# Gate products of a recurrence one product later, and a Newton step in two operations

## The chip, the cores and the metric

The kernel runs on one core of a Trainium2 chip. The metric is the device time of one execution in microseconds, as the median of several runs. A core has TensorE (PE, matrix products into PSUM banks), VectorE (DVE), ScalarE (ACT), GpSimd (POOL) and SyncE (SP), which here only starts DMAs. Each engine works through its own queue in program order; semaphores tie the queues together.

## The reference

One layer of a decoder block on x of 2048 positions by 1024 features, in float32:

```python
proj = x @ w_in + b_in        # 1024 -> 9216 columns: q, k, v, g_attn, u_lru, g_lru, two merge gates
attn = combined(dilated_band_attention(rope(q), rope(k), v)) * silu(g_attn)   # three dilation groups
y_a  = attn @ w_attn_proj
u    = causal_depthwise_conv(u_lru, conv_w, conv_b)     # width 4
h    = rg_lru(u, ...)                                    # below
y_b  = (h * silu(g_lru)) @ w_lru_proj
out  = (sigmoid(gA) * y_a + sigmoid(gB) * y_b) @ w_out + b_out
x    = layer_norm(2 ** 0.25 * x + out, ln_gain, ln_bias)
```

The recurrence, with block-diagonal 64 x 64 gate weights:

```python
r = sigmoid(u @ w_r + b_r);  i = sigmoid(u @ w_i + b_i)
a = exp(-8 * r * softplus(-lam))
h[t] = a[t] * h[t-1] + sqrt(1 - a[t]**2) * i[t] * u[t]
```

## The kernel before

Every float32 product is made of three matmuls in the reduced-precision form `float32r`: an operand is split into a high part (ScalarE copies it into that form) and the rest (VectorE subtracts), and high x high, high x low and low x high are summed in PSUM.

**Stages.** The kernel runs four stages: the input projection with everything that can be done on its columns (to about 1446 us), attention (to about 1659 us), the projection of the recurrence's branch, and the attention projection with the output projection and LayerNorm (to the end).

**The input projection.** It is computed by Strassen's scheme (Winograd's form): two column tiles (of 128 columns) against two position chunks (of 512) make a *unit* of seven products instead of eight. There are 36 units in each half of the positions; `plan` lists them, and `seq` gives the order of kinds ("qk", "v", "ug" for the recurrence's input and its gate, "ga", "mg"). A product is 12 matmuls of 128 x 512 at line 622 and fills one PSUM bank `q`, of which there are four (line 615). The usual order of the products is `MID`, by their ids 1, 6, 7, 5, 2, 4, 3. After each product `evacuate` reads its bank: id 1 is copied by ScalarE to `e`; id 6 gives `u = e - q`, id 7 `v = u + q`, id 5 gives an output from `v` and then `u = u + q`, and ids 2, 4 and 3 give the other outputs. The weights' sums S1 to S4 (`add_w`, `sums`, `sum3`) and their splits (`prep_w`, writing `h` and `l`) are issued at fixed products ahead of use, their loads (`load_w`, line 234) earlier still.

**The chains.** What happens to an output afterwards is a Python generator, started in `result`: `qk_chain` (rotary, split, stores at lines 330, 341 and 344, with four DMAs at line 307 for the swapped halves), `v_chain`, `silu_chain`, `mg_chain` and `lru`. A chain yields `Ask(lag=.., need=.., keep=.., cond=.., ACT=.., DVE=..)`: its next step is issued `lag` products later at the earliest, when enough of the 32 slots of 128 x 512 are vacant, the condition holds, and the planner's budget of each named engine (2.75 us for every product) is not used up. The order that results in each queue is fixed when the program is built. `pe_later(n, fn)` puts matmuls of a chain into the middle of the product n on (line 625).

**The recurrence.** `lru(i, c, ub)` handles block i (of 8) and chunk c (of 4), 32 chains in all. It computes the convolution `v`, splits it into `vh` and `vl` (lines 482 and 483, the latter recorded under line 227), and two products later asks for the gates: `gates` issues six matmuls on half the rows each (line 492) into two banks `g`. Then follow the tanh of both gates on ScalarE, the coefficients, and the scan (line 527). `gate["busy"]` lets one chain at a time be between its gates and its tanh, and `gate["live"]` lets two chains be between convolution and scan.

**LayerNorm.** `out_job(tt)` handles 128 positions: the output product (lines 1415 to 1417), the residual, mean and variance, and then r = 1/sqrt(var + eps): ScalarE takes the root, VectorE the reciprocal (line 1443), and one Newton step r <- r * (1.5 - 0.5 * (var + eps) * r * r) corrects it, on one column of 128 values (lines 1445 to 1448). The two halves of the tile are then scaled, shifted (line 1452) and stored.

Of the kernel before, what the change touches and what calls it, by code (L numbers as in the profile page):

```python
# [11 lines left out]
ALU = mybir.AluOpType  # L12
# [19 lines left out]
def hybrid_block_kernel(ctx: ExitStack, tc: tile.TileContext, a: dict, out: bass.AP):  # L32
    nc = tc.nc
    sp, act, dve, pool, pe = nc.sync, nc.scalar, nc.vector, nc.gpsimd, nc.tensor
# [62 lines left out]
    def pe_later(lag, fn):  # L97
        pe_late.append((now["n"] + lag, fn))
# [348 lines left out]
    def lru(i, c, ub):  # L447
# [19 lines left out]
        for j in range(1, 4):  # L467
            dve.scalar_tensor_tensor(out=v, in0=ub[:, j:j + CH], scalar=lrn[:, j, i:i + 1], in1=v,
                                     op0=ALU.mult, op1=ALU.add)
# [24 lines left out]
            if c in ((0, 3) if i in put_off else (1, 3)):  # L494
                give(GW[i])

        pe_later(1, gates)
        gated[i] = c + 1
        yield Ask(lag=2, need=2, keep=1, ACT=2.5)
        gate["busy"] = False  # L500
        tr, ti = take("tr" + nm, F32), take("ti" + nm, F32)
        for h, (hs, os) in enumerate((HALF, HALF[::-1])):
# [69 lines left out]
    def result(s, fi, c, bank, u):  # L572
# [10 lines left out]
        if kind in ("qk", "v"):  # L583
            y = take("y" + nm)
            total(flat(y), bank, u, f, sgn, True)
            start_chain(qk_chain(y, f, c) if kind == "qk" else v_chain(y, sgn, f, c))
        elif kind == "mg":
            y = take("y" + nm, F32)
            total(y, bank, u, f, sgn, False)
            start_chain(mg_chain(y, sgn, f, c))  # L590
        elif kind == "ga" or not fi:
            y = take("y" + nm, F32)
            total(y, bank, u, f, sgn, False)
            start_chain(silu_chain(y, sgn, f, c))
        else:
            i = f - FT_U
            if c == 1 and i in put_off:
                y = take("y" + nm, F32)
                total(y, bank, u, f, sgn, True)
                act.activation(ubs[:, i, 2, 0:3], y[:, CH - 3:CH], AF.Copy)  # L600
                start_chain(store_chain(y, u_scr[i]))
                return
            ub = ub_free.pop(0)
            total(ub[:, 3:3 + CH], bank, u, f, sgn, True)
            start_chain(lru(i, c, ub), 7 if c % 2 else 0)
# [100 lines left out]
    for s, pl in enumerate(plan):  # L706
        if pl[4] == "ug" and not (pl[0] and pl[1][1][0] - FT_U in put_off):
            at(base[s] + 1, lambda i=pl[1][1][0] - FT_U: fetch_gr(i))
        if pl[0] and pl[4] == "ug":
            i = pl[1][1][0] - FT_U  # L710
            if i not in put_off:
                continue
            at(base[s] - 12, lambda i=i: start_chain(lru(i, 1, None)))
# [677 lines left out]
    def load_xr(tt):  # L1391
        XR[tt] = vx_p.tile([P, D], F32, tag="x", name=f"x{tt}", bufs=3)
        sp.dma_start(XR[tt], a["x"][tt * P:(tt + 1) * P, :])

    def split_m(tt, ks=slice(0, 8)):
        c, b = divmod(tt, 4)
        m = ME[c][:, ks, b * P:(b + 1) * P]
        if ks.start == 0:
            MS[tt] = tuple(vx_p.tile([P, 8, P], F32R, tag=t, name=f"{t}{tt}", bufs=2) for t in ("mh", "ml"))
        mh, ml = (t[:, ks] for t in MS[tt])  # L1400
        act.activation(mh, m, AF.Copy)
        dve.tensor_tensor(out=ml, in0=m, in1=flat(mh), op=ALU.subtract)

    def out_job(tt):
        rows = slice(tt * P, (tt + 1) * P)
        x = XR.pop(tt)
        mh, ml = MS.pop(tt)
        last = tt == 15
        parts = [slice(0, CH), slice(CH, CH + 256), slice(CH + 256, D)] if last else [slice(0, CH), slice(CH, D)]
        zz = [fp.tile([P, CH], F32, tag="z", name=f"z{tt}{n}", bufs=3)[:, 0:hs.stop - hs.start] for n, hs in enumerate(parts)]  # L1410
        for k0, k1 in ((0, 6), (6, 8)) if tt == 0 else ((0, 8),) if tt % 4 else ((0, 7), (7, 8)):
            for z, hs in zip(zz, parts):
                for k in range(k0, k1):
                    w = WO[k]
                    pe.matmul(z, mh[:, k], w[:, 0, hs], start=(k == 0), stop=False)  # L1415
                    pe.matmul(z, mh[:, k], w[:, 1, hs], start=False, stop=False)  # L1416
                    pe.matmul(z, ml[:, k], w[:, 0, hs], start=False, stop=(k == 7))  # L1417
        if tt + 1 < 16:
            load_xr(tt + 1)
            split_m(tt + 1, slice(0, 8 if (tt + 1) % 4 else 7))  # L1420
        if tt == 1:
            for fn in at1:
                fn()
        dve.scalar_tensor_tensor(out=x, in0=x, scalar=ALPHA, in1=vec[0], op0=ALU.mult, op1=ALU.add)
        st_ = cst.tile([P, 4, 6], F32, tag="st", name=f"st{tt}", bufs=2)
        n = 0
        for z, hs in zip(zz, parts):
            dve.tensor_tensor(out=x[:, hs], in0=x[:, hs], in1=z, op=ALU.add)
            step = 256 if last else CH
            for q in range(hs.start, hs.stop, step):  # L1430
                dve.bn_stats(out=st_[:, n, :], in_=x[:, q:q + step])
                n += 1
        mv = cst.tile([P, 4], F32, tag="mv", name=f"mv{tt}", bufs=2)
        dve.bn_aggr(out=mv[:, 0:2], in_=st_[:, 0:n])
        act.activation(mv[:, 2:3], mv[:, 1:2], AF.Sqrt, bias=epst)
        halves = (slice(0, CH), slice(CH, D))

        def centre(hs):
            dve.scalar_tensor_tensor(out=x[:, hs], in0=x[:, hs], scalar=mv[:, 0:1], in1=vec[1][:, hs],
                                     op0=ALU.subtract, op1=ALU.mult)  # L1440

        centre(halves[0])
        dve.reciprocal(out=mv[:, 2:3], in_=mv[:, 2:3])

        dve.tensor_scalar(out=mv[:, 1:2], in0=mv[:, 1:2], scalar1=EPS, scalar2=-0.5, op0=ALU.add, op1=ALU.mult)
        dve.tensor_tensor(out=mv[:, 3:4], in0=mv[:, 2:3], in1=mv[:, 2:3], op=ALU.mult)
        dve.tensor_scalar(out=mv[:, 3:4], in0=mv[:, 3:4], scalar1=mv[:, 1:2], scalar2=1.5, op0=ALU.mult, op1=ALU.add)
        dve.tensor_tensor(out=mv[:, 2:3], in0=mv[:, 2:3], in1=mv[:, 3:4], op=ALU.mult)
        for hs, eng in zip(halves, (sp, act) if last else (act, act)):
            if hs.start:  # L1450
                centre(hs)
            dve.scalar_tensor_tensor(out=x[:, hs], in0=x[:, hs], scalar=mv[:, 2:3], in1=vec[2][:, hs],
                                     op0=ALU.mult, op1=ALU.add)
            eng.dma_start(out[rows, hs], x[:, hs])
# [26 lines left out]
    for tt in range(16):  # L1481
        c, b = divmod(tt, 4)
        run(late)
        out_job(tt)
        if c + 1 < NCH:
            for f in (((0, 1), (2, 3), (4, 5, 6), (7,)) if c else ((), (0, 1, 2), (3, 4, 5, 6), (7,)))[b]:
                ya_job(8 * (c + 1) + f)
            if b == 3:
                split_m(tt + 1, slice(7, 8))
                bring_at(c + 2)  # L1490
        now["n"] += 1
# [59 lines left out]
```

## Time and profile before

| what | value |
|---|---|
| runs | 2118.34, 2118.59, 2121.45 us; median 2118.59 |
| profiled execution | 2117.73 us, its span 2116.0 us |
| granted TensorE clock, mean | 0.999 |
| TensorE busy | 2083.6 us, 98% of the span |
| VectorE busy | 1667.7 us, 79% |
| ScalarE busy | 1123.4 us, 53% |
| GpSimd busy | 490.1 us, 23% |
| DMA | 524.69 MB, 248 GB/s on average |

The span runs from the first to the last instruction of the profiled execution; the execution's own time has 1.73 us more. In the timeline rows a line reads: start, duration (both us), engine, line of the kernel, operation, output<-inputs, shapes, count, and in brackets the idle time before it with what ended it. `PEld` is TensorE's weight load and overlaps its matmuls; `SPq` is SyncE's queue, whose rows are DMAs being started. Matmuls are pipelined, so the starts of successive ones are closer than their durations.

### The profile page before, as it was taken

To read this page: it belongs to the slowest core of one execution; us is meant where nothing else is said; L and a number is where in the kernel's file an instruction comes from. 1 tells how busy PE (TensorE), PEld (TensorE's weight loads), DVE (VectorE), ACT (ScalarE), POOL (GpSimd) and SP (SyncE) were. 2 spreads that over 40 slices of the span, in tenths; PEclk is the share of its full clock that TensorE was granted. 3 is DMA by queue.
4 is the path that set the end of the run, shared out by engine and by line. 5 is a ranking of instruction groups with operands and counts; after the bars stand their busy time and mean duration, and the time that the engine had idled before them with its cause. 6 is when DMAs were issued, how large, how long until landed. Compare 5 with 4: busy or idle time off the path is not lost.

```text
span 2116.0 us, 35899 instructions
## 1 busy us (share of the span) xinstructions
PE 2083.6 (98%) x12016; PEld 1723.9 (81%) x12016; DVE 1667.7 (79%) x3193; ACT 1123.4 (53%) x2348; POOL 490.1 (23%) x465
## 2 busy tenths in 40 slices
PE   8999999999999999999999999999999999999998
PEld 7888888888878888887888888888888888888887
DVE  8987888898888867787787887777999645576667
ACT  6356455357356565656567766667999411121100
POOL 1111111111111012231231232223535444332120
PEclk9999999999999999999999999999999999999999
DMA  8987997997997977677788788879988788874432
GB/s 271 280 259 225 281 277 212 285 288 230 276 289 230 331 219 202 214 238 211 249 255 269 255 254 265 259 224 383 293 305 260 227 278 282 293 250 158 164 110 70
DMA packets 345832, 524.69 MB, mean 248 GB/s; under 512 B 124208, under 2 KB 153904, under 8 KB 341808
## 3 DMA queue, kind: packets, MB, share of 16 engines
q1 hardware_dynamic: 325760, 489.54, 71.3%
q0 software_dynamic: 12256, 19.42, 5.6%
q10 hardware_dynamic: 7632, 13.44, 1.7%
q8 instruction: 96, 1.57, 0.3%
q14 instruction: 88, 0.72, 0.1%
HBM read 317.14 MB, written 190.45 MB: 240 GB/s over the span
## 4 chain that ended last, share of the span: by engine, by line
PE 64%; ACT 5%; DVE 3%; DMA 1%; issue 1%; SPq 0%; DVEq 0%; ACTq 0%
PE q L622 39%; ACT p L1020 3%; PE yb L1305 3%; PE yb L1306 3%; PE z L1415 3%; PE z L1416 3%; PE yb L1307 3%; PE z L1417 3%; PE ya L1383 1%; PE ya L1384 1%; PE ya L1385 1%; PE o L1058 1%; DVE p L1012 1%; ACT ptb L1043 1%; PE g L492 1%; PE s L1005 1%
## 5 line engine op out<-in xcount | busy, mean ns | idle before, releaser
L622 PE MATMUL q<-xT,hS 128*128 128x512 f32 x1680 | 521.1, 391 | 0.0
L622 PE MATMUL q<-xT,l 128*128 128x512 f32 x1120 | 436.0, 389 | 0.0
L622 PE MATMUL q<-xB,hA 128*128 128x512 f32 x1248 | 389.5, 393 | 5.7 <-ACT xB L215 5.7
L622 PEld LDWEIGHTS q<-xT,hS 128*128 128x128 f32 x1680 | 312.8, 188 | 69.0 <-issue 5.5
L622 PE MATMUL q<-xB,l 128*128 128x512 f32 x904 | 353.0, 391 | 0.0
L622 PEld LDWEIGHTS q<-xB,hA 128*128 128x128 f32 x1248 | 234.0, 189 | 57.2 <-ACT xB L215 5.7
L622 PEld LDWEIGHTS q<-xT,l 128*128 128x128 f32 x1120 | 210.2, 188 | 44.2
L622 PEld LDWEIGHTS q<-xB,l 128*128 128x128 f32 x904 | 170.4, 188 | 36.0
L245 POOL DMA_DIRECT2D wS<-in_w_in_dram x70 | 62.0, 969 | 493.7 <-DMA wS<-in_w_in_dram 139.0
L1020 ACT ACTIVATE p<-p,sta 128x256 f32<-128x256 f32 (+1 forms) x384 | 172.2, 456 | 4.8 <-DVE sta L1012 4.1
L622 PE MATMUL q<-xB,hS 128*128 128x512 f32 x560 | 174.1, 392 | 0.0
L622 PE MATMUL q<-xT,hA 128*128 128x512 f32 x560 | 173.0, 390 | 0.0
L269 ACT ACTIVATE hA<-wA 128x512 fp32r<-128x512 f32 x218 | 134.9, 623 | 53.2 <-DMA wA<-in_w_in_dram 23.8
L269 ACT ACTIVATE hS<-S 128x512 fp32r<-128x512 f32 x175 | 109.0, 623 | 79.4 <-DVE S L227 51.1
L227 POOL TENSOR_TENSOR S<-S,wA 128x512 f32<-128x512 f32 x35 | 45.5, 1299 | 392.8 <-DVE S L227 218.0
L622 PEld LDWEIGHTS q<-xT,hA 128*128 128x128 f32 x560 | 104.7, 188 | 23.0 <-issue 1.5
L622 PEld LDWEIGHTS q<-xB,hS 128*128 128x128 f32 x560 | 104.0, 188 | 22.4 <-issue 1.5
L1012 DVE CUSTOM_DVE_ANT_0 p<-s,mask 128x256 f32<-128x256 f32 (+1 forms) x384 | 118.7, 360 | 4.3 <-PE s L1005 3.3
L1416 PE MATMUL z<-wo,mh 128*128 128x512 f32 (+1 forms) x264 | 101.0, 383 | 0.0
L1417 PE MATMUL z<-wo,ml 128*128 128x512 f32 (+1 forms) x264 | 101.0, 383 | 0.0
L1415 PE MATMUL z<-wo,mh 128*128 128x512 f32 (+1 forms) x264 | 101.0, 383 | 0.0
L1305 PE MATMUL yb<-h,wl 128*128 128x512 f32 x256 | 100.3, 392 | 0.0
(201 smaller groups left out, 4208.5 us busy)
## 6 DMA issues: line engine op xcount, KB each, us to landing
wA<-in_w_in_dram SPq DMA_DIRECT2D x253, 256.0 KB, 4.8
wl_scr<-l SPq DMA_DIRECT2D x105, 512.0 KB, 5.2
l<-wl_scr SPq DMA_DIRECT2D x105, 512.0 KB, 4.7
sw<-y SPq DMA_DIRECT2D x384, 64.0 KB, 3.2
wS<-in_w_in_dram SPq DMA_DIRECT2D x70, 256.0 KB, 4.9
wS<-in_w_in_dram POOLq DMA_DIRECT2D x70, 256.0 KB, 6.2
qh_scr<-hi SPq DMA_DIRECT2D x48, 256.0 KB, 5.7
v_scr<-vs SPq DMA_DIRECT2D x48, 256.0 KB, 4.4
```

What stands on the lines that cost most here:

```text
L227: eng.tensor_tensor(out=out, in0=in0, in1=in1, op=op)
L245: pool.dma_start(t, w_part(s, x), accum_op=ALU.add)
L269: act.activation(h, r, AF.Copy)
L622: pe.matmul(bank, w[:, ks], x[:, kk, xx], start=(first and i == 0), stop=(last and i == 11))
L1012: dve.tensor_tensor_reduce(out=st["p", i, j][:, h, lo:256], in0=st["s", i, j // 2][h][:, j % 2, lo:256], in1=mask[:, lo:256], scale=1.0, s ...
L1020: act.activation(p, p, AF.Exp, scale=-1.0, bias=s[:, h:h + 1], accum_out=s[:, 2 + h:3 + h])
L1305: pe.matmul(yb, WL[f][:, 0, k], xx[:, 0], start=(k == 0), stop=False)
L1306: pe.matmul(yb, WL[f][:, 0, k], xx[:, 1], start=False, stop=False)
L1307: pe.matmul(yb, WL[f][:, 1, k], xx[:, 0], start=False, stop=(k == 7))
L1415: pe.matmul(z, mh[:, k], w[:, 0, hs], start=(k == 0), stop=False)
L1416: pe.matmul(z, mh[:, k], w[:, 1, hs], start=False, stop=False)
L1417: pe.matmul(z, ml[:, k], w[:, 0, hs], start=False, stop=(k == 7))
```

## The change

```diff
-        pe_later(1, gates)
+        pe_later(2, gates)
         gated[i] = c + 1
-        yield Ask(lag=2, need=2, keep=1, ACT=2.5)
+        yield Ask(lag=3, need=2, keep=1, ACT=2.5)
...
         dve.tensor_scalar(out=mv[:, 1:2], in0=mv[:, 1:2], scalar1=EPS, scalar2=-0.5, op0=ALU.add, op1=ALU.mult)
-        dve.tensor_tensor(out=mv[:, 3:4], in0=mv[:, 2:3], in1=mv[:, 2:3], op=ALU.mult)
-        dve.tensor_scalar(out=mv[:, 3:4], in0=mv[:, 3:4], scalar1=mv[:, 1:2], scalar2=1.5, op0=ALU.mult, op1=ALU.add)
-        dve.tensor_tensor(out=mv[:, 2:3], in0=mv[:, 2:3], in1=mv[:, 3:4], op=ALU.mult)
+        dve.scalar_tensor_tensor(out=mv[:, 3:4], in0=mv[:, 2:3], scalar=mv[:, 2:3], in1=mv[:, 1:2], op0=ALU.mult, op1=ALU.mult)
+        dve.tensor_scalar(out=mv[:, 2:3], in0=mv[:, 3:4], scalar1=1.5, scalar2=mv[:, 2:3], op0=ALU.add, op1=ALU.mult)
```

In `lru`, the gate matmuls go into the middle of the second product after the request instead of the first, and the tanh that reads them is asked for three products after it instead of two. Every later step of the chain follows from there. In `out_job`, three operations on one column become two: (r * r) * (-0.5 * (var + eps)) in one, and (that + 1.5) * r in the other.

## The prediction

> **What bounds the kernel now.** I read the page's busy times first, then TensorE's own waits, then the timeline around the one wait that names the gates, then the timeline of the last tile.
>
> ```profile
> span 2116.0 us, 35899 instructions
> ## 1 busy us (share of the span) xinstructions
> PE 2083.6 (98%) x12016; PEld 1723.9 (81%) x12016; DVE 1667.7 (79%) x3193; ACT 1123.4 (53%) x2348; POOL 490.1 (23%) x465
> ```
>
> TensorE is busy for 2083.6 of 2116.0 us, so all its idle time together is 32.4 us. An edit that removes no matmul can only win from that. The waits of TensorE say where most of it lies:
>
> ```profile
> PE o L1058 <- ACT ptb L1043: 13.9, 43, 0.6
> PE q L622 <- ACT xB L215: 5.7, 1, 5.7
> PE pt L1030 <- ACT p L1020: 1.5, 7, 0.2
> PE g L492 <- DVE vl L227: 1.5, 1, 1.5
> ```
>
> The columns are total us, times, longest. The 13.9 and 1.5 us of L1058 and L1030 belong to attention, which the diff leaves alone; the 5.7 us is one wait for the first input block. What the gates cost by waiting is one event of 1.5 us: only one of the 32 gate products found its operand `vl` late. The rest of the recurrence's shift therefore has nothing to win on TensorE, and can only lose. A measurement of this kernel can tell about 0.2% from no change, 4.2 us of 2118.59; the event is a third of that.
>
> **The gates, step 1: what an undisturbed gate product costs.** It is put into the middle of a product, so its cost is read from start to start on TensorE:
>
> ```profile
> 428.00 0.39 PE L622 MATMUL q<-xB,l 128*128 128x512 f32 x1
> 428.32 0.50 PE L492 MATMUL g<-vh,gw 64*128 64x512 f32 x2
> 428.65 0.40 PE L492 MATMUL g<-vl,gw 64*128 64x512 f32 x2
> 428.89 0.40 PE L492 MATMUL g<-vh,gw 64*128 64x512 f32 x2
> 429.21 0.73 PE L622 MATMUL q<-xB,hS 128*128 128x512 f32 x2
> 429.79 0.39 PE L622 MATMUL q<-xB,l 128*128 128x512 f32 x1
> 430.02 0.63 PE L622 MATMUL q<-xB,hS 128*128 128x512 f32 x2
> 430.48 0.39 PE L622 MATMUL q<-xB,l 128*128 128x512 f32 x1
> ```
>
> A plain matmul follows the one before it after 0.23 us (429.79 to 430.02). Here the six gate matmuls put 1.21 us between 428.00 and 429.21, 0.98 more than that; and the next pair takes 0.58 us (429.21 to 429.79) where a pair takes 0.46 (430.02 to 430.48), 0.12 more. A gate product thus costs 1.10 us, wherever it stands. Moving 32 of them by one product changes nothing in that term: 32 x 1.10 before and after, cost of the move itself 0. The six matmuls are all that the moved step issues; it starts no DMA.
>
> **Step 2: what the stall really costs.**
>
> ```profile
> 583.67 0.39 PE L622 MATMUL q<-xB,l 128*128 128x512 f32 x1
> 583.99 0.50 PE L492 MATMUL g<-vh,gw 64*128 64x512 f32 x2
> 585.97 0.50 PE L492 MATMUL g<-vl,gw 64*128 64x512 f32 x2 [1.48 <-DVE vl L227]
> 586.31 0.39 PE L492 MATMUL g<-vh,gw 64*128 64x512 f32 x2
> 586.63 0.73 PE L622 MATMUL q<-xB,hS 128*128 128x512 f32 x2
> ...
> 588.13 0.62 PE L622 MATMUL q<-xB,hA 128*128 128x512 f32 x2
> ```
>
> From 583.67 to 586.63 is 2.96 us against 1.21 undisturbed: 1.75 us lost, a little more than the 1.48 that the row shows as idle. This product is the last of its unit of seven (`xB,hS` is the product with S4); the first of the next unit (`xB,hA`) starts at 588.13.
>
> **Step 3: what is late next.** The reason for the stall is in VectorE's and SyncE's queues:
>
> ```profile
> 578.65 0.68 DVE L227 TENSOR_TENSOR v<-u,q 128x512 f32<-128x512 f32 x1
> 584.02 0.69 DVE L227 TENSOR_TENSOR S<-S,wA 128x512 f32<-128x512 f32 x1 [4.69 <-DMA wA<-in_w_in_dram]
> 584.63 0.68 DVE L227 TENSOR_TENSOR l<-wA,hA 128x512 fp32r<-128x512 f32 x1
> 585.23 0.69 DVE L227 TENSOR_TENSOR vl<-v,vh 128x512 fp32r<-128x512 f32 x1
> 585.83 0.68 DVE L227 TENSOR_TENSOR y<-q,v 128x512 f32<-128x512 f32 x1
> 586.43 0.68 DVE L227 TENSOR_TENSOR u<-u,q 128x512 f32<-128x512 f32 x1
> ```
>
> ```profile
> 570.72 4.78 SPq L341 DMA_DIRECT2D ql_scr<-rp  x1
> 575.59 3.61 SPq L330 DMA_DIRECT2D k_scr<-rp  x1
> 579.25 0.42 SPq L234 DMA_DIRECT2D wA<-in_w_in_dram  x1
> ```
>
> SyncE spent 8.4 us on issuing two stores of the q/k chains, so a weight load went out at 579.25 and VectorE sat idle 4.69 us for it at the head of its queue. Behind that stood `l`, then `vl`, then the two reads `y<-q,v` and `u<-u,q`. These two empty the bank of the unit's fourth product (id 5 of the order 1, 6, 7, 5, 2, 4, 3). There are four q banks, so the first product of the next unit, four products on, writes that same bank. It comes free at 586.43 + 0.68, plus the 0.05 us by which the gate at 585.97 followed the end of `vl` (585.92): 587.16.
>
> With the gates out of the last product, its second half follows at 583.90 and takes six matmuls of 0.227 us: the next unit would start at 585.26 and find its bank not yet free. It would wait 1.90 us, to 587.16, and only then pay the gates' 1.10 in its middle. Set against 588.13, where the gates are already paid, that is 587.16 + 1.10 - 588.13 = 0.13 us later. So of the 1.75 us nothing comes back as long as VectorE is as late as now: the wait moves from `vl` to the bank. The gates themselves would then find `vl` long done.
>
> The Trainium skill's page "PSUM — Partial Sum Buffer", section "Engine vs sequencer instructions", says that VectorE's queue is strictly first in, first out. The rows agree: from 578.65 to 584.02 nothing passed the waiting add, although `y<-q,v` had its product. By that rule the term is +0.13 us; could VectorE take the bank's reads ahead of the late add, the term would be the whole -1.75.
>
> The bounds of this term are -1.75 (VectorE is less late here, because the nine earlier recurrence chains of this half also shifted) and +0.13 (nothing but the gates moved). I take +0.13: it is worked out from rows at the place itself, and the two long stores are those of the q/k chains, which the diff does not touch.
>
> **Step 4: the longer chains.** Each chain gets one product longer, some 2.7 us: `vh` and `vl` hold two of the 32 slots for one product more, and the tanh, the scan and the store come one product later. The tanh is still issued one product after its gates, so ScalarE waits no longer for TensorE than now: 0. The chain that ends last:
>
> ```profile
> 1410.92 1.28 DVE L527 TENSOR_TENSOR_SCAN h<-tr,hst,sq 128x512 f32<-128x512 f32 x1
> ```
>
> TensorE works on the input projection until about 1445, so even two products more (block 7's two chains follow each other) end this scan near 1418: covered, 0. Were that cover gone, a chain's VectorE work would fall into attention. What cannot be read off is the order that results: the planner hands VectorE's and ScalarE's time out product by product, so other chains' steps swap places with those of the recurrence. Its price is bounded below by -1.75, the only stall there is to lose, and above by one more q/k store ahead of a weight load, +3.61. I take 0, because with the present order one of 32 gate products and no q product after the first stalled.
>
> **Step 5: the Newton step.** Only the last tile's counts, since TensorE waits for nothing of LayerNorm in the others.
>
> ```profile
> 2109.84 0.16 DVE L1443 RECIPROCAL mv<-mv 128x1 f32<-128x1 f32 x1
> 2109.91 0.13 DVE L1445 TENSOR_SCALAR mv<-mv 128x1 f32<-128x1 f32 x1
> 2110.03 0.16 DVE L1446 TENSOR_TENSOR mv<-mv 128x1 f32<-128x1 f32 x1
> 2110.22 0.21 DVE L1447 TENSOR_SCALAR mv<-mv 128x1 f32<-128x1 f32 x1
> 2110.47 0.16 DVE L1448 TENSOR_TENSOR mv<-mv 128x1 f32<-128x1 f32 x1
> 2110.67 0.75 DVE L1452 SCALAR_TENSOR_TENSOR x<-x,mv,vec 128x512 f32<-128x512 f32 x1
> ```
>
> From L1445 to L1452 is 0.76 us now. Dependent operations start 0.03 to 0.04 us after the end of the one before; L1446 did not depend on L1445 and started before its end. The new fused operation does: it takes L1445's result as its second tensor, so that overlap is lost. No fused operation on one column with a scalar from memory is in the trace. The 512-column form takes 0.75 (L1452) against 0.68 for two tensors without such a scalar (585.83 above), so I add 0.07 to L1446's 0.16: 0.23, with 0.16 and 0.30 as ends. Then 0.13 + 0.04 + 0.23 + 0.04 + 0.21 (as L1447) + 0.04 = 0.69: a gain of 0.07 us, between 0.00 and 0.14.
>
> **The sum.** The profiled execution took 2117.73 us, 1.73 outside its span, and lies 0.86 below the median of the runs, 2118.59. Gates +0.13, order 0, Newton step -0.07: 2117.79 for that execution, 2118.65 for the median. I say 2118.6.
>
> **The rivals.**
> - *The stall goes and nothing takes its place.* For it: nine chains have shifted by then, so VectorE and SyncE need not meet the load in this state. Against: the two long stores and the weight load belong to other work. 2118.59 - 1.75 - 0.07 = 2116.8.
> - *The new order makes a stall of its own.* VectorE's lateness turns up at another gate product or bank. One like the present one on top of the bank's wait gives 2118.65 + 1.75 = 2120.4; one 3.61 us store before a load, 2122.2.
> - *Slower.* The place is the bank of the unit's fourth product, as in step 3. It is already the bound there, so each us that the load at 579.25 slips is one us for TensorE. If the shifted order puts one more store like the 4.78 us one in front of it, the time is 2118.65 + 4.78 = 2123.4. It decides from a slip of 4.2 us. Against: by then another load would have to be late as well as this one.
> - *Faster by over 0.2%.* That needs 4.2 us of TensorE's idle time; beyond the 1.75 the diff touches no place that has it.
>
> **How the numbers follow.** Wait moves to the bank, no change: 0.42. Stall gone: 0.20. A stall elsewhere, up to 3.6 us: 0.22. Slower by over 0.2%: 0.12. Faster by over 0.2%: 0.04. The first three are within 0.2%: 0.84. The range runs from the stall gone with 0.14 for the Newton step, in an execution as far below the median as the profiled one (2118.59 - 1.75 - 0.14 - 0.86 = 2115.8), to one more store of 3.61 us (2122.2); the slower case and the faster one lie outside, 0.16 together.
>
> **What would show it.** Right: no wait of the gates for `vl`; in its place, near 585, a wait of a q product for VectorE's `u` of about 1.9 us; about 0.7 us from L1445 to L1452 in the last tile; gate rows with the same spacing, one product later. Wrong: no wait of TensorE at all in that stretch (the stall gone), or waits of q products or gates for VectorE at other places (the new order), or a last scan beyond 1440.

## The result and the profile after

The changed kernel takes 2131.35 us (median of 6 runs, 2130.94 to 2133.28) against 2119.69 for the kernel before (6 runs, 2117.88 to 2122.74): 1.0058 of its time, 95% interval 1.0047 to 1.0068. It is 11.7 us slower, and the prediction (2118.6, range 2115.8 to 2122.2) was wrong. The profiled execution of the changed kernel took 2130.94 us, its span is 2128.9.

The page's busy times after:

```profile
span 2128.9 us, 35908 instructions
## 1 busy us (share of the span) xinstructions
PE 2088.3 (98%) x12016; PEld 1723.6 (81%) x12016; DVE 1667.9 (78%) x3177; ACT 1123.5 (53%) x2348; POOL 493.3 (23%) x465
```

The span grew by 12.9 us. TensorE has the same 12016 matmuls; its busy time grew by 4.7 us (2083.6 to 2088.3) and its idle time by 8.2 (32.4 to 40.6). The busy time of VectorE and ScalarE is what it was, though the gates' chains were moved on both.

TensorE's waits after (us in total, times, longest):

```profile
PE o L1058 <- ACT ptb L1043: 14.2, 43, 0.6
PE q L622 <- DMA l<-wl_scr: 6.5, 3, 4.8
PE q L622 <- ACT xB L215: 5.6, 1, 5.6
PE pt L1030 <- ACT p L1020: 1.5, 7, 0.2
PE q L622 <- DVE u L227: 1.2, 1, 1.2
PE z L1417 <- DVE ml L1402: 0.8, 1, 0.8
...
PE g L492 <- ACT ti L504: 0.5, 1, 0.5
```

The gates' 1.5 us for `vl` are gone, a wait of 1.2 us for `u` has come, as forecast, and then there is a line that the profile before does not have: three waits, 6.5 us together, for the DMA that brings the low parts `l` of the weights. TensorE's timeline shows the longest of them:

```profile
1288.78 0.61 PE L622 MATMUL q<-xB,hS 128*128 128x512 f32 x2
1294.19 0.80 PE L622 MATMUL q<-xB,l 128*128 128x512 f32 x1 [4.79 <-DMA l<-wl_scr]
1294.78 1.05 PE L622 MATMUL q<-xB,hS 128*128 128x512 f32 x2
...
1299.47 0.59 PE L622 MATMUL q<-xB,l 128*128 128x512 f32 x1
1299.90 0.62 PE L622 MATMUL q<-xB,hA 128*128 128x512 f32 x2
```

The wait is not all. From 1294.19 to 1299.90 stand 13 matmuls in 5.71 us; at the usual 0.227 they take 2.95. The missing 2.8 us are in the clock. The view by stretches of 5 us gives, per engine, busy us and count (PE, PEld, DVE, ACT, POOL), then granted clock, DMA share and GB/s:

```profile
1285.00:1290.00 5.00, 4.40 (x20) 3.31 (x18) 0.78 (x2) 0.00 (x0) 0.00 (x0) 1.00 0.81 267
1290.00:1295.00 5.00, 0.81 (x2) 0.72 (x3) 4.10 (x6) 2.75 (x5) 2.96 (x3) 0.81 0.95 300
1295.00:1300.00 5.00, 5.00 (x13) 3.84 (x13) 5.00 (x7) 2.04 (x4) 1.68 (x1) 0.51 0.74 146
1300.00:1305.00 5.00, 5.00 (x24) 4.10 (x23) 3.74 (x5) 3.97 (x8) 0.00 (x0) 1.00 1.16 326
```

Half the clock for five microseconds, behind an idle time of 4.8. This explains most of the 4.7 us by which busy TensorE grew. The Trainium skill's page "TensorE: Matmul & The Clock Gate", section "Part 1: The HAM clock gate", says that the clock falls to half after an idle window of about 3.4 us and comes back after about as long a busy stretch. The rows agree with the fall: 0.51 behind 4.79 us of idle time, while the clock stayed at 1.00 behind waits of 0.71 and 1.01 us. Full speed came back after 13 matmuls here, 5.71 us, later than that figure of the Trainium skill.

**Where the time went.** Set the start of one and the same matmul in both traces side by side. The changed kernel is 0.1 us ahead at the start. Up to unit 61 (1231 us) its distance moves up and down, at the units' starts between 1.3 ahead and 1.4 behind, in part since the 1.10 us of each gate product now fall one product later; unit 61 starts 1.1 behind. Unit 62 starts 2.15 behind, unit 64 9.85, and unit 65 and the end of the input projection are 11.6 behind. Through attention and the recurrence's projection it is 11.6 to 11.8. The last stage adds 1.1, of which 0.8 is the wait of `z` for `ml`; that wait also stands in kernels below that are no slower, so it is not the change. So nearly the whole loss arises between 1238 and 1309 us, late in the second half of the input projection.

**Why the low parts were late.** They are loaded by SyncE, one instruction after the other. SyncE's queue after:

```profile
1281.84 0.53 SPq L344 DMA_DIRECT2D qh_scr<-hi  x1
1282.46 0.38 SPq L344 DMA_DIRECT2D ql_scr<-rp  x1
1282.93 3.40 SPq L307 DMA_DIRECT2D sw<-y  x4
1286.42 2.17 SPq L234 DMA_DIRECT2D wA<-in_w_in_dram  x2
1288.65 0.42 SPq L330 DMA_DIRECT2D k_scr<-rp  x1
1289.17 1.39 SPq L287 DMA_DIRECT2D l<-wl_scr  x3
```

and before:

```profile
1278.77 2.01 SPq L287 DMA_DIRECT2D l<-wl_scr  x2
1280.87 0.59 SPq L341 DMA_DIRECT2D qh_scr<-hi  x1
1281.55 3.40 SPq L341 DMA_DIRECT2D ql_scr<-rp  x1
1285.05 1.36 SPq L330 DMA_DIRECT2D k_scr<-rp  x1
1286.50 1.11 SPq L287 DMA_DIRECT2D l<-wl_scr  x2
```

After the change, SyncE works through the q/k chains' DMAs and the weights from 1281.8, with one pause of 1.2 us (inside the row at 1286.42) that its list of waits puts down to the landing of `wo_scr`, and three loads of low parts go out together from 1289.17. TensorE had run out of them at about 1289.24 (1288.78 and two matmuls of 0.23): the load was issued as it was needed, and TensorE sat through its way from memory. From issue to landing such a load takes 3.6, 4.7, 9.2 us (least, median, most) in the trace before. Its lead, from issue to first use, I worked out for every load: in unit 63 it was 10.5, 9.8, 7.0 and 7.7 us before, and 9.0, 5.6, 4.0 and 5.0 after. The last two of these contain the 1.01 and 4.79 us that TensorE stood waiting for them.

VectorE ran late as well. The first rows are after, the others before: the last matmul of unit 63's second product, and the row of VectorE that empties its bank.

```profile
1276.38 0.39 PE L622 MATMUL q<-xT,l 128*128 128x512 f32 x1
1282.13 0.68 DVE L227 TENSOR_TENSOR u<-e,q 128x512 f32<-128x512 f32 x1
```

```profile
1273.83 0.39 PE L622 MATMUL q<-xT,l 128*128 128x512 f32 x1
1275.62 0.68 DVE L227 TENSOR_TENSOR u<-e,q 128x512 f32<-128x512 f32 x1
```

From the end of the product (start + 0.39) to `u<-e,q` are 5.4 us after and 1.4 before. For the units 60 to 63 this lateness is 2.4, 0.1, 2.2, 1.4 us before and 6.1, 2.5, 6.6, 5.4 after: VectorE runs some 4 us behind where it ran.

In unit 61 the trace shows a place where VectorE loses time: the third product's read, `v<-u,q`, first after, with the store that it waits for, then before.

```profile
1238.80 0.53 SPq L410 DMA_DIRECT2D ga_scr<-y  x1
1246.82 0.69 DVE L227 TENSOR_TENSOR v<-u,q 128x512 f32<-128x512 f32 x1 [4.40 <-DMA ga_scr<-y]
```

```profile
1239.97 0.68 DVE L227 TENSOR_TENSOR v<-u,q 128x512 f32<-128x512 f32 x1
```

After, VectorE stands idle for 4.40 us until the store of a `g_attn` output has landed, 7.9 us after its issue. In the program's own order `v` takes the slot from which that store reads, in the very product in which it becomes vacant. Before, the row waits for nothing.

### The profile page after: what moved, and what is told of

Its sections match the earlier page's. It is cut to its first block, busy times and chain, and to the rows that moved or that the text cites. A ratio compares the mean times of both kernels' runs of the same rounds, so it can differ in the third digit from the quotient of the medians.

```text
span 2128.9 us, 35908 instructions
## 1 busy us (share of the span) xinstructions
PE 2088.3 (98%) x12016; PEld 1723.6 (81%) x12016; DVE 1667.9 (78%) x3177; ACT 1123.5 (53%) x2348; POOL 493.3 (23%) x465
```

## The experiments

The runs of a group shared a chip with fresh runs of the kernel before; each ratio is against those.

**Which part of the change.** First the parts alone: the Newton step; the gates' two lines; and of those only the place of the matmuls, with the tanh asked for as early as before.

```diff
 e1: only the three lines of out_job
 e2: only the two lines of lru
 e3:
-        pe_later(1, gates)
+        pe_later(2, gates)
         yield Ask(lag=2, need=2, keep=1, ACT=2.5)
```

> The Newton step in two operations alone, the gates as before. Both theories: 0.0 to 0.14 us less than before, which the runs cannot tell from no change (ratio 0.999 to 1.001); TensorE waits as before, with its one wait for vl near 585. If the Newton step had a part in the 12 us, at least 2 us would show here.

> The gates' two edits alone, the Newton step as before. Both theories: all of the slowdown, 2130 to 2133 us, with TensorE waiting three times for the low weight parts between 1245 and 1300 us.

> The gates in the second product after the request, but the tanh still asked for two products after it: the chains are no longer than before, and only the place of the gates on TensorE and the time for which vh and vl hold their two slots are those of the change. Theory 1 (the longer chains crowd the later queues and SyncE starts the loads of the low weight parts too late): 2118 to 2121 us, no wait of TensorE for those loads. Theory 2 (the place of the gates on TensorE, or the two slots held a product longer, is what costs): 2126 to 2132 us.

Measured: the Newton step 2118.91 us, 0.9995 [0.9986, 1.0004]; the gates' lines 2132.62, 1.0062 [1.0042, 1.0083]; the place alone 2117.57, 0.9992 [0.9981, 1.0003]. TensorE's waits with the place alone:

```profile
PE o L1058 <- ACT ptb L1043: 13.6, 42, 0.6
PE q L622 <- ACT xB L215: 5.7, 1, 5.7
PE pt L1030 <- ACT p L1020: 1.5, 7, 0.2
PE z L1417 <- DVE ml L1402: 0.8, 1, 0.8
```

Neither a wait for `vl` nor one for `l`. Issuing the gates one product later costs nothing that can be measured; what costs 0.6% is `lag=3` (e2 against e3), by which the tanh, the coefficients, the scan and the store of every chain come one product later. VectorE's lateness in units 60 to 63 is 1.8, 0.8, 0.6, 0.6 us in e3.

**The loads themselves.** If the loads are simply issued too late, asking for them one product earlier should help.

```diff
 e7, on the changed kernel:
-                at(t0 + j - 1, lambda s=s, j=j: load_lo(s, j))
+                at(t0 + j - 2, lambda s=s, j=j: load_lo(s, j))
```

> The changed kernel with the loads of the low weight parts asked for one product earlier (t0 + j - 2), in a queue that is otherwise the same in kind. Theory 1: a load that stood 4.0 to 5.0 us ahead of its use stands some 2.7 us earlier, so the waits of 0.7, 1.0 and 4.8 us and the slow clock behind the last one shrink or vanish: 2120 to 2125 us. Theory 2: the loads are only where the lateness is seen, another operand is late next, and the time stays at 2128 to 2132 us.

2129.76 us, 1.0042 [1.0029, 1.0056]. One wait of 3.7 us for `l` is left and 2.2 us of waits for `u` have come; VectorE is as late as before (7.8, 4.2, 6.3, 5.0). About a quarter of the loss goes back: most of it does not come from the place of these loads in the queue alone.

**SyncE blocked by the gate branch's stores.** The `mg` stores go out on SyncE in this stretch and may wait there at the head of the queue.

```diff
 e8, on the changed kernel (the stores from ScalarE's queue from then on):
-        if base[len(seq) - 2] + 3 <= now["n"] < base[len(seq) + 2]:
+        if base[len(seq) - 2] + 3 <= now["n"]:
```

> The changed kernel with the merge gates' stores of the second half started from ScalarE's queue, right behind their tanh, instead of from SyncE's; SyncE then never stands at such a store waiting for the tanh (10.3 us of such waits between 1240 and 1300 us). Theory Q (SyncE's queue, blocked at those stores, is what makes the loads of the low weight parts late): the waits of TensorE for these loads vanish, 2119 to 2124 us. Theory S (the shortage of slots makes VectorE wait for a store that still reads the slot, and all else follows): most of it stays, 2126 to 2132 us.

2131.82 us, 1.0066 [1.0051, 1.0081]; 6.0 us of waits for `l`, three as before, the longest 4.2. That theory fell. The rival in the same expectation, a shortage of slots that makes VectorE wait for a store which still reads its slot, had 2126 to 2132 us.

**The slots.** `vh` and `vl` hold two of 32 slots for one product longer, and by the program's own count at the end of each product the fewest vacant slots in the second half are 0 after (product 430, in unit 61; 1 at 432 and 433) and 2 before. Three runs: a 33rd slot, paid for with one of the two buffers `vs`, with and without the change; and one slot fewer in the kernel before.

```diff
 e9 (changed kernel), e10 (kernel before):
-    NS, NL = 32, 4
+    NS, NL = 33, 4
-    vs_free = [... for j in range(2)]
+    vs_free = [... for j in range(1)]
 e11 (kernel before):
-    NS, NL = 32, 4
+    NS, NL = 31, 4
```

> The changed kernel with 33 slots instead of 32; the room comes from the second buffer for the transposed v, of which one is left. Theory S: slots are reused one turn later, VectorE's wait of 4.4 us near 1242 for a store out of a slot goes, and the loads come in time: 2119 to 2124 us. Theory Q: 2128 to 2133 us, with TensorE still waiting for the low weight parts.

> The same exchange in the kernel before, as the control: both theories 2117 to 2121 us; a difference from the kernel before by more than 4 us would mean that the single v buffer or the slots' rotation matters by itself.

> The kernel before, gates and chains as they were, with 31 slots. By the planner's own count the vacant slots go down to none at products 180, 236 and 486 to 493, as they do at 430 to 433 in the changed kernel. Theory S: waits of VectorE for stores and late operands appear at such places without any change to the gates, 2123 to 2132 us. Theory Q: 2118 to 2122 us.

With 33 slots: 2140.5 us, 1.0108 [1.0088, 1.0128] with the change and 2135.72, 1.0080 [1.0065, 1.0095] without. The buffer given away costs more than the question is worth: 7.3 us of waits of `vtp` for it in both. The change on top costs about 0.28% there instead of 0.58%, and VectorE's lateness in units 60 to 63 is 0.8, 0.7, 1.4 and 2.6 us with the change, as small as without it; but with a kernel so disturbed this is a hint and no answer. One slot fewer before: 2127.49, 1.0042 [1.0026, 1.0059], and here the place differs from that of the change:

```profile
PE s L1005 <- DVE sta L1012: 6.5, 1, 6.5
```

The input projection ends only 1.06 us later, without any wait for `l`; the loss comes where attention starts and finds VectorE behind. Scarce slots can cost this much, but these runs don't show that they are what costs it here.

The traces say more. In the six with a wait of 3.7 us or more for `l` (the changed kernel, e2, e7, e8, f1 and g2), the row `v<-u,q` of unit 61 starts 4.6 to 6.9 us after the end of its product, each time 0.1 us behind the landing of that `ga` store. In the other twelve it starts at most 2.4 us after its product, and no such store holds it. This goes with the lateness of units 62 and 63; no run changes this slot alone.

**Two chains at a time, and a longer chain elsewhere.** A third chain between convolution and scan would give back throughput if that limit were the matter. And if any longer chain did it, one product more ahead of the scan, in the kernel before, would do the same.

```diff
 f1, on the changed kernel:
-        ... cond=lambda: gate["live"] < 2 and begun[i] == c, ...
+        ... cond=lambda: gate["live"] < 3 and begun[i] == c, ...
 f3, on the kernel before:
-            yield Ask(need=1, keep=1, DVE=1.6, cond=lambda: done[i] == c)
+            yield Ask(lag=2, need=1, keep=1, DVE=1.6, cond=lambda: done[i] == c)
```

> The changed kernel with three chains of the recurrence allowed between convolution and scan instead of two. Theory D (in the changed kernel VectorE has done 4 to 9 us less work than in the kernel before by the same product from unit 45 to 64, because each chain is a product longer, and runs late when it catches up; everything that waits for it, SyncE's stores and the loads behind them, runs late too). If it is the limit of two chains that puts the work off: 2118 to 2124 us. If the work is put off by the lag and the vacant slots alone: 2127 to 2135 us.

> The kernel before with its gates as they were; only the scan is asked for two products after the step ahead of it instead of one, so each chain is one product longer at its last step. Theory D: it is the chains' length, not the gates, that costs: 2124 to 2135 us. Rival (what costs is the gap between gates and tanh or the hold of vh and vl): 2117 to 2121 us.

f1: 2132.5 us, 1.0064 [1.0050, 1.0078], and 6.3 us of waits for `l`: the limit isn't it. (`lag=3` also keeps `gate["busy"]` set for a product longer; in the program's own order this holds no chain back, before or after.) f3: 2124.8, 1.0022 [1.0012, 1.0033]. It lost 1.4 us up to the end of the input projection and then 4.3 us at attention's start, with VectorE late in units 60 to 63 by 2.9, 0.6, 2.0, 3.2. A longer chain costs, but how much and where depends on the step that is put off.

**VectorE relieved.** If the loads come late because VectorE, and what SyncE's queue waits for from it, runs late, work taken off VectorE must remove the stall. f4 computes one of the weights' sums on GpSimd (35 operations on 128x512, all in the second half); g4 does the same in the kernel before.

```diff
-        tt(dve, t, t, raw[s, "A11"], ALU.add)
-        spend(DVE=.9)
+        tt(pool, t, t, raw[s, "A11"], ALU.add)
+        spend(POOL=1.4)
```

> The changed kernel with the weight sum S3 of the second half's 35 units on GpSimd instead of VectorE, 35 x 0.69 = 24 us less work for VectorE there. Theory D: VectorE is less late in units 60 to 63 (6.1, 2.5, 6.6, 5.4 us after its product there, against 2.4, 0.1, 2.2, 1.4 before), and the loads come in time: 2117 to 2124 us. Rival (SyncE's queue is late by itself): 2127 us or more.

> The kernel before with S3 of the second half on GpSimd, the control of the same edit in the changed kernel: 2115 to 2121 us, since VectorE's lateness there costs TensorE nothing in the kernel before. If it came out at 2124 us as well, the edit would have shown nothing of the cause.

f4: 2124.79 us, 1.0025 [1.0016, 1.0034]. g4: 2121.85, 1.0019 [1.0010, 1.0029]. Moving the sum thus costs 0.19% by itself, and with it in place the change adds about 0.06%, which the two intervals (some 0.13% either way) don't tell from nothing, instead of 0.58%. TensorE's waits in f4:

```profile
PE q L622 <- ACT xB L215: 5.7, 1, 5.7
PE q L622 <- DVE u L227: 2.1, 1, 2.1
...
PE g L492 <- ACT ti L504: 0.9, 1, 0.9
```

The waits for `l` are down to 0.4 us, and VectorE's lateness is 2.0, 0.1, 2.8, 2.2, as without the change. In g4 one wait of 1.9 us for `l` appears, so these loads have little to spare there too. The edit also changes what the planner issues when: in f4 the `ga` stores of this stretch are out by 1222.3, and `v<-u,q` of unit 61 doesn't wait for one. So the stall goes together with VectorE's lateness, but f4 does not tell less work from another order.

**Which chains.** The longer lag for the first half of the positions alone, for the second alone, and only for the two chains of block 5 that run ahead of the stall.

```diff
+        far = now["n"] < base[36]      # g1;  g2: >= base[36];  g3: i == 5 and c >= 2
-        pe_later(2, gates)
+        pe_later(2 if far else 1, gates)
-        yield Ask(lag=3, need=2, keep=1, ACT=2.5)
+        yield Ask(lag=3 if far else 2, need=2, keep=1, ACT=2.5)
```

> The gates' two edits for the chains of the first half of the positions' units alone. If the loss is that of units 62 to 64: 2118 to 2122 us, at most the 1 to 3 us that the drift shows up to unit 30. If the first half's order carries over into the second: over 2125 us.

> The gates' two edits for the chains issued in the second half alone. If the loss is made there: 2127 to 2132 us with the waits for the low weight parts in units 62 to 64. If it needs the first half's shift: 2118 to 2122 us.

> The gates' two edits for two chains alone, block 5 with chunks 2 and 3; these are the ones whose tanh, coefficients and scan run while units 60 to 63 are prepared. Local theory (the two chains' VectorE work, moved by one product, lands on the preparation of these units): 2124 to 2132 us, with TensorE waiting for the low weight parts. Theory of the accumulated deficit (4 to 9 us of VectorE's work put off since unit 45): 2117 to 2122 us and no such wait.

g1: 2122.16 us, 1.0019 [1.0009, 1.0028]. g2: 2126.94, 1.0036 [1.0022, 1.0049]. Together 0.55%, the whole within its interval. g2's waits (its lines count one more from 497 on):

```profile
PE q L623 <- DMA l<-wl_scr: 5.8, 2, 4.3
...
PE g L492 <- DVE vl L227: 1.4, 1, 1.4
```

The old wait for `vl` (a chain of the first half) is back, and the wait for `l` has stayed, with VectorE late by 6.1, 2.5, 6.4, 5.2: the big stall belongs to the second half's chains alone. The first half has no such wait; its input projection ends 2.1 us later, part of it where a chain's gates wait for the tanh of the chain ahead to free the two banks `g`:

```profile
498.68 0.50 PE L492 MATMUL g<-vh,gw 64*128 64x512 f32 x1 [0.18 <-ACT ti L505]
500.09 0.50 PE L492 MATMUL g<-vh,gw 64*128 64x512 f32 x1 [0.91 <-ACT ti L505]
```

g3: 2120.25 us, 1.0010 [1.0001, 1.0020], with 1.6 us of waits for `l` and VectorE late by 2.8, 1.1, 1.6, 3.6. Two chains alone bring a small part of the stall; most of it needs the shift of the whole half. (The 0.19% of the first half, which f4's edit does not touch, should have stayed in f4; its 0.06% just reaches there within the intervals.)

**A version from the parts that cost nothing.** The gates one product later, the tanh as early as before, and the new Newton step (the change with `lag=2`).

> The gates in the second product after the request, the tanh still two products after it, and the Newton step in two operations: the parts of the change that did not lengthen the chains. All theories: as the gates' place alone, 2116 to 2119 us, ratio 0.998 to 1.000, with no wait of TensorE for vl.

2119.4 us, 1.0001 [0.9992, 1.0010]. No kernel here is measurably faster than the one before.

## Why the prediction was wrong

**Step 1 (a gate product costs 1.10 us wherever it stands): held.** e3 moves all 32 of them and takes 0.9992 of the time, an interval that includes no change.

**Steps 2 and 3 (the wait goes from `vl` to the bank): held in kind.** TensorE after, at the place the prediction named:

```profile
586.37 0.39 PE L622 MATMUL q<-xB,l 128*128 128x512 f32 x1
587.96 0.70 PE L622 MATMUL q<-xB,hA 128*128 128x512 f32 x2 [1.21 <-DVE u L227]
...
589.51 0.50 PE L492 MATMUL g<-vh,gw 64*128 64x512 f32 x2
589.85 0.40 PE L492 MATMUL g<-vl,gw 64*128 64x512 f32 x2
```

The first product of the next unit waits 1.21 us for `u` (forecast 1.9), and the gates behind it wait for nothing. Nothing came back, as worked out.

**Step 4 (the longer chains: taken as 0): this is the step that failed.** It is the term that measured about 11.7 us. Its first half held: the last scan starts at 1424.9, under 1440, and is covered. But the cover was looked up for that one scan, at the end of the stage, whereas the long stall came some 130 us ahead of it, at 1289. The second half, "I take 0, because with the present order one of 32 gate products and no q product after the first stalled", took the absence of waits as a sign of room. Waits are zero as long as a load lands before its use, however little time is left. The lead itself was in the trace: at unit 56 a low part was issued 5.9 us ahead of its use, with a landing of 4.7 us in the median and 9.2 at most. I read the loads of `wA` on SyncE and never those of `l`, which stand in the same queue. The step also named the two slots that are held a product longer and set no price on scarcer slots. e3 holds these two as long and loses nothing; with the whole chain longer the slots run out at product 430, and VectorE stands 4.40 us for one.

The upper bound, "one more q/k store ahead of a weight load, +3.61", was too low in two ways. It let one thing go wrong once, while a step put off in 16 chains of a half moves what VectorE and SyncE do in every unit. And it priced a stall by its wait alone: here 4.79 us of idle time brought 2.8 us of slow clock behind them.

**Step 5 (Newton step): held.** The last tile after:

```profile
2122.74 0.16 DVE L1443 RECIPROCAL mv<-mv 128x1 f32<-128x1 f32 x1
2122.82 0.14 DVE L1445 TENSOR_SCALAR mv<-mv 128x1 f32<-128x1 f32 x1
2122.99 0.22 DVE L1446 SCALAR_TENSOR_TENSOR mv<-mv 128x1 f32<-128x1 f32 x1
2123.24 0.21 DVE L1447 TENSOR_SCALAR mv<-mv 128x1 f32<-128x1 f32 x1
2123.49 0.75 DVE L1451 SCALAR_TENSOR_TENSOR x<-x,mv,vec 128x512 f32<-128x512 f32 x1
```

From L1445 to the scaling (now L1451) are 0.67 us, forecast 0.69; the fused operation takes 0.22, forecast 0.23. The gain of 0.09 us is far below what a measurement of the whole can tell.

**The rivals.** The slower rival had the right sign and the wrong place: it put the stall at 585, on the bank and a load of `wA`; it came at 1289, on a load of `l`. The rival of an order with a stall of its own had the right mechanism and stopped at 3.6 us.

**What is shown, and what is not.** Shown: `lag=3` causes the loss (e2 against e3, with e1 for the rest of the change), about two thirds of it in the second half (g1, g2); there TensorE waits for low parts that SyncE issues too late, and loses clock behind the wait; the stall and VectorE's lateness go together, and with a sum of the second half moved off VectorE both go, and most of the cost with them (f4 against g4). Excluded as sources: the gates' place, the place of the loads alone, the `mg` stores, the limit of two chains. Argued from the traces, and not shown by a run that changes only this: VectorE is late in units 62 and 63 because in unit 61 it waits for a slot that a store still reads, which fits the program's count of 0 vacant slots one product earlier. Open: why VectorE is already 6.1 us late in unit 60, ahead of that wait, where it was 2.4 before.

## What to carry to other kernels

A profile without waits does not say how far an order can be pushed: before moving a step that many chains share, read for each in-order queue the least lead of its loads (issue to first use) and compare it with their landing time. A step put off by one product holds its buffers longer and moves the work of everything planned after it, so its bound is the tightest lead in the stage, not the end of the moved chain. Look also for the product at which the fewest buffers are vacant: there an engine can stand at the head of its queue for a store that still reads the buffer. Price a TensorE stall of several microseconds at more than its length.

## What the runs showed of the hardware

After 4.79 us without a matmul the granted clock was 0.51 in the next five microseconds, and 13 matmuls took 5.71 us instead of 2.95; waits of 0.71 and 1.01 us left it at 1.00. Behind the longest waits for `l` in e2, e7, e8, f1 and g2, of 3.72 to 4.91 us, 13 matmuls took 4.67 to 5.62 us. Stalls of this length thus cost 1.7 to 2.8 us more than the profile's waits say.
